# Edge key blocks in a hybrid attention trunk: products over 128 query columns instead of 256 with zeros

## The chip, the cores and the metric

The kernel runs on one core of one Trainium2 chip, in one launch. The metric is the device time of that core in microseconds (us), from the first instruction of the program to the last; lower is better. Five engines and the DMA queues matter in the text: TensorE (PE in the profile, its weight loads listed apart as PEld), VectorE (DVE), ScalarE (ACT), GpSimd (POOL), and SyncE (SP, which issues nearly all DMAs).

## What is computed

The reference is a trunk of two layers over 1024 tokens of width 1024, in float32. Each layer projects the normalised input to three groups of attention heads that run beside each other, normalises each group's output, multiplies by one output matrix and adds the result to the stream; a SwiGLU feed-forward part follows.

```
def reference(...):
    for l in range(2):
        h = rms_norm(x, g_attn[l]) * (1 + sc_a) + sh_a
        qa, ka, va, qb, kb, vb, qc, kc, vc = split_cols(h @ w_in[l], IN_SPLITS)
        ya = neighborhood_attention(qa, ka, va, rpb_na[l])         # 4 heads, 8 x 16 window on a 16 x 64 grid
        yb = sliding_window_attention(qb, kb, vb, sink_sw[l], t5)  # 6 heads, |i - j| <= 128
        yc = axial_attention(qc, kc, vc, gq_ax[l], gk_ax[l])       # 6 heads, dense
        y = concat([rms_norm(ya), rms_norm(yb), rms_norm(yc)])
        x = x + gt_a * (y @ w_o[l])
        h = rms_norm(x, g_ffn[l]) * (1 + sc_f) + sh_f
        gate, up = split_cols(h @ w_gu[l])
        x = x + gt_f * ((silu(gate) * up) @ w_down[l])
    return rms_norm(x, g_final)
```

In the neighbourhood group a query sees 8 grid rows of 64 tokens around its own, so a block of 128 queries (two grid rows) sees up to 9 rows, 576 keys. In the sliding group a block of 128 queries sees its own block of 128 keys and one block on either side, as far as there is one.

## The kernel before, in words

Products of float32 numbers are made from parts of type F32R: a number is rounded to a high part on ScalarE (`act.copy` into an F32R tile), and VectorE or GpSimd subtracts it from the original to get the low part. Such a pair is multiplied in two or three matmuls. Every matmul in the trace comes with a weight load of its own.

In a layer's attention part the work goes in pairs of query blocks: 24 pairs of the dense group C (6 heads by 4 pairs), 16 of the neighbourhood group A (4 heads by 4 pairs) and 24 of the sliding group B (6 heads by 4 pairs), in that order, in the list `stream`. Each pair, of 256 queries, goes through three steps:

- `qk`: the scores in PSUM (tiles `sC`, `sA`, `sB`), on VectorE the bias and the row's extreme (tile `rs`), on ScalarE the exponential with its sum (tile `pr`), then a reciprocal on VectorE and a scaling of the row on GpSimd;
- `turn`: blocks of 128 keys by 128 queries are transposed on TensorE into a PSUM tile `T`, from which `split_pt` makes the high and the low part (ScalarE, then VectorE) in the tiles `pt`;
- `pv`: for each key block `kc`, `products` multiplies the values `vs[:, kc]` as weights with the transposed rows as moving columns, the high and the low part one after the other, and adds up in a PSUM tile `pv` (two pairs share its 512 columns).

Most key blocks are seen by both query blocks of a pair, and their tiles hold 256 columns. An edge key block is seen by one of the two only: the key block before the pair by its left query block, the one behind by its right. In the neighbourhood group the two inner pairs of each head have two edge blocks (`PairA`, `self.inner`); in the sliding group pairs 1 and 2 of each head have two, pairs 0 and 3 one (`PairB`, `self.left`, `self.right`). These parts lie in tiles called `edge`. Before the change there are two `edge` tiles for the whole part, made once by `edges_make` with 256 columns for each side: the columns of the query block that does not see the key block are set to zero by GpSimd and stay so, and `next_edge` hands out the two tiles in turn. So every matmul of an edge block has 256 moving columns, as the others have.

With 2 matmuls (high and low) for each edge block there are 16 edge blocks in the neighbourhood group (32 matmuls) and 36 in the sliding group (72 matmuls) of a layer: 104, and 208 in the kernel.

In the attention part only GpSimd's instructions stand in the order of the source (`pin((pool,), True)`). For TensorE, VectorE, ScalarE and SP the order is laid down by the scheduler of the framework when the kernel is built, from its own picture of when each instruction is ready. Another shape of a few matmuls can therefore move other instructions too. All operations are issued through one helper, so that the profile gives line 49 for nearly all of them; the tiles' names tell them apart.

Of the kernel before, what the change touches and what calls it, by code (L numbers as in the profile page):

```python
# [76 lines left out]
def f32(ap):  # L77
    return ap.bitcast(F32)
# [7 lines left out]
def trunk(ctx: ExitStack, tc, A, C, out):  # L86
# [723 lines left out]
    for l in range(2):  # L810
# [379 lines left out]
        zA = [zA_tile() for _ in range(2)]  # L1190
        zB = [bz_tile() for _ in range(2)]
        gss = {23: gss_tile()}
        edge = []

        def edges_make():
            for _ in range(2):
                e = atp.tile([P, 2, 2, 256], F32R, name="edge", tag="edge", bufs=2)
                for z in range(2):
                    pool.memset(f32(e[:, z, 0, 128:256]), 0.0)
                    pool.memset(f32(e[:, z, 1, 0:128]), 0.0)  # L1200
                edge.append(e)

        edges_used = [0]

        def next_edge():
            edges_used[0] += 1
            return edge[edges_used[0] % 2]

        def edge_ap(e, z, left, right):
            flat = e[:, z, :, :].rearrange("p e q -> p (e q)")  # L1210
            if left and right:
                return flat.rearrange("p (a q) -> p a q", a=4)[:, 0:4:3, :]
            return flat[:, None, 0:128] if left else flat[:, None, 384:512]

        def pt_tile():
            return wp.tile([P, 4, 256], F32R, name="pt", tag="whl", bufs=8)
# [14 lines left out]
        class Pair:  # L1231
# [11 lines left out]
            def products(self, movs, part):  # L1243
                if part == 0:
                    if self.p % 2 == 0:
                        open_pv[0] = psV.tile([P, H], F32, name="pv", tag="V")
                    self.pvt = open_pv[0]
                cols = slice((self.p % 2) * 256, (self.p % 2) * 256 + 256)
                half = (len(movs) + 1) // 2
                for n, (kc, a, b) in enumerate(movs):  # L1250
                    if (n < half) != (part == 0):
                        continue
                    for i, mv in enumerate((a, b)):
                        pe.matmul(
                            self.pvt[:, cols], vs[:, kc, self.vh, :], mv,
                            start=(n == 0 and i == 0), stop=(n == len(movs) - 1 and i == 1),
                        )
                if part and self.p % 2:
                    self.combine()
# [68 lines left out]
        class PairA(Pair):  # L1328
# [64 lines left out]
            def pv(self, part):  # L1393
                k0 = {0: 0, 1: 1, 2: 3, 3: 4}[self.p]
                movs = [(k0 + i, self.pt[0][:, i, :], self.pt[1][:, i, :]) for i in range(4)]
                if self.inner:
                    e = self.e
                    movs.append((k0 - 1, e[:, 0, 0, :], e[:, 1, 0, :]))
                    movs.append((k0 + 4, e[:, 0, 1, :], e[:, 1, 1, :]))
                self.products(movs, part)  # L1400

        class GroupB:
# [18 lines left out]
        class PairB(Pair):  # L1421
# [64 lines left out]
            def pv(self, part):  # L1486
                k0, e = 2 * self.p, self.e
                movs = [(k0 + i, self.pt[0][:, i, :], self.pt[1][:, i, :]) for i in range(2)]
                if self.left:
                    movs.append((k0 - 1, e[:, 0, 0, :], e[:, 1, 0, :]))  # L1490
                if self.right:
                    movs.append((k0 + 2, e[:, 0, 1, :], e[:, 1, 1, :]))
                self.products(movs, part)


# [93 lines left out]
        for n in range(-AHEAD - 1, N + 1):  # L1589
            ahead = AHEAD if n + AHEAD < 40 else AHEAD_B  # L1590
            begin = range(done, min(n + ahead + 1, N))
            for i in range(2):
                if 0 <= n < N:
                    pairs[n].turn(i)
                while unfinished:
                    unfinished.pop(0)()
                if 0 <= n - 1 < N:
                    pairs[n - 1].pv(i)
                for m in begin:
                    if m < made:  # L1600
                        pairs[m].qk(i)
            done = max(done, min(begin.stop, made))
            while made < min(N, n + ahead + 2):
                for key, make in preload.get(made, []):
                    heads[key] = make()
                pairs[made] = stream[made][0]()
                made += 1
            for what in later.pop(n, []):
                what()
            if n == 50:  # L1610
                yq = qk_tile()
            if n == 8:
                edges_make()
            if n == 54:
                wst = [w_o_stage(k) for k in korder[:2]]
            if n in (55, 59):
                ki = (n - 55) // 4
                y_split(korder[ki], 0, yq[:, ki, 0:H], yq[:, ki, H:S])
            if n in (59, 61):
                w01.append(split_tile(wst.pop(0), 1, (atp, "pr", 6), dve))  # L1620
            if n == 60:
                t2 = [psS.tile([P, 2, H], F32, name="ps_o", tag="S") for _ in range(2)]
                pss = [t2[i // 2][:, i % 2, :] for i in range(NS)]
            if n in (61, 62):
                o_rows(0, w01[0], range(NS)[2 * (n - 61) : 2 * (n - 60)])
            if n in (63, 64):
                o_rows(1, w01[1], range(NS)[2 * (n - 63) : 2 * (n - 62)])
            if n == 62:
                wq = [w_rows(w_o, k * P, eng=dve) for k in korder[2:4]]
            m = n - 1  # L1630
            for end, (chunks, width) in norms.items():
                if begins[end] <= m <= end and (m - begins[end]) % 8 == 7:
                    i = (m - begins[end]) // 8
                    if end not in gss:
                        gss[end] = gss_tile()
                    for half in range(2):
                        what = lambda a=(chunks, gss[end], i, half): norm_sum(*a)
                        if m == N - 1:
                            what()
                        else:  # L1640
                            later.setdefault(n + 1 + half, []).append(what)
                    if m == end and end < N - 1:

                        def stats(end=end, width=width, n=n, chunks=chunks):
                            r = rstd_cols([gss[end]], width, 8, atp, psT, tag="T", newton=True)

                            def scale():
                                todo = norm_scale(chunks, r, psT, "T", (pool, pool))
                                for i, what in enumerate(todo):
                                    later.setdefault(n + 9 + i, []).append(what)  # L1650

                            later.setdefault(n + 8, []).append(scale)

                        later.setdefault(n + 5, []).append(stats)
# [693 lines left out]
```

## Time and profile before

| | |
|---|---|
| median of 3 runs | 2460.08 us (2459.95 to 2464.16) |
| profiled execution, its own time | 2460.14 us |
| its span, first to last instruction | 2458.4 us |
| TensorE busy | 2387.5 us, 97% |
| VectorE busy | 1819.2 us, 74% |
| ScalarE busy | 1227.1 us, 50% |
| GpSimd busy | 764.6 us, 31% |

A TensorE record covers a matmul's way through the array, so that records of neighbouring matmuls overlap. How fast matmuls follow each other is read from the distance of their starts (or of their ends, where the first of a group waited), not from the length of one record. Busy TensorE is therefore not TensorE at its limit.

In both layers the attention part runs at the same places of the program. By the first and the last record of the score tiles, the neighbourhood group's scores lie at 368 to 429 us of the span in the first layer and 1573 to 1633 us in the second, the sliding group's at 429 to 495 us and 1634 to 1699.5 us; products of both groups run on a little behind the scores, the last until 513 and 1717 us.

### The profile page before, as it was taken

The page shows a single profiled execution, that of the slowest core. Times are in us where ns is not written, and L with a number is a line of the kernel's source. Part 1 is how long each engine was busy: PE and PEld are TensorE (multiplying, and loading weights), DVE is VectorE, ACT ScalarE, POOL GpSimd, SP SyncE. Part 2 cuts the span into 40 slices and gives each one's busy share as a digit, 9 for nine tenths or more (in the row PEclk, how much of TensorE's full clock was granted, in tenths as well). Part 3 has the DMA queues.
Part 4 walks back from the last instruction along what each step waited for, and adds up shares of the span by engine and source line. Part 5 has one row for each costly group of instructions (what it writes and reads, how often), then busy time and mean ns, then how long its engine had stood idle before and what let it go on. Part 6 is the DMA issues. An engine that isn't in the chain of part 4 may idle for free.

```text
span 2458.4 us, 34300 instructions
## 1 busy us (share of the span) xinstructions
PE 2387.5 (97%) x12005; PEld 1991.2 (81%) x12005; DVE 1819.2 (74%) x2966; ACT 1227.1 (50%) x2306; POOL 764.6 (31%) x769
## 2 busy tenths in 40 slices
PE   8999999999999999999999999999999999999998
PEld 4787899878788787788787789987887888888886
DVE  5757999986967888586677679998688545446865
ACT  3422888954543333344543148888444343334443
POOL 1520445620244444300036124465004434430001
PEclk9999999999999999999999999999999999999999
DMA  8468205255245454596424851141624332229743
GB/s 285 149 188 282 56 6 145 57 165 160 86 142 173 158 178 152 163 274 193 152 85 116 279 165 27 48 148 50 206 86 141 119 121 95 99 96 296 209 134 110
DMA packets 285205, 356.04 MB, mean 145 GB/s; under 512 B 32996, under 2 KB 201532, under 8 KB 285032
## 3 DMA queue, kind: packets, MB, share of 16 engines
q1 hardware_dynamic: 277816, 341.12, 44.4%
q10 hardware_dynamic: 6912, 12.59, 1.6%
q8 instruction: 95, 1.56, 0.3%
q14 instruction: 78, 0.64, 0.1%
q0 software_dynamic: 304, 0.14, 0.0%
HBM read 269.62 MB, written 86.69 MB: 145 GB/s over the span
## 4 chain that ended last, share of the span: by engine, by line
PE 73%; DVE 9%; DMA 6%; issue 4%; ACT 4%; POOL 2%; SPq 1%; ACTq 0%; POOLq 0%; DVEq 0%
PE ps_w L49 28%; PE ps_d L49 14%; PE ps_o L49 7%; PE pv L49 6%; PE ps_ab L49 6%; PE T L49 4%; PE sC L49 3%; DMA wmt<-in_w_mod_dram 1%; SPq L49 1%; ACT pr L49 1%; DMA zAd<-zt 1%; PE sA L49 1%; DMA zt<-skA 1%; PE ps_v L49 1%; PE ps_c L49 1%
## 5 line engine op out<-in xcount | busy, mean ns | idle before, releaser
L49 PE MATMUL ps_d<-wpt 128*128 128x512 f32 x1848 | 424.3, 390 | 2.4 <-ACT wpt L49 2.1
L49 PEld LDWEIGHTS ps_d<-wpt 128*128 128x128 f32 x1848 | 345.6, 188 | 76.4 <-issue 3.0
L49 POOL TENSOR_SCALAR pr<-pr,rs 128x1024 f32<-128x1024 f32 (+4 forms) x252 | 206.9, 823 | 309.8 <-DVE rs L49 293.2
L49 POOL TENSOR_TENSOR sg<-sg,u 128x512 f32<-128x512 f32 x86 | 124.6, 1451 | 356.3 <-ACT sg L49 117.9
L49 PE MATMUL pv<-pt,vs 128*128 128x256 f32 x1216 | 202.0, 296 | 7.8 <-DVE rs L49 2.3
L49 DVE TENSOR_TENSOR pt<-T,pt 128x512 fp32r<-128x512 f32 x304 | 199.5, 680 | 11.4 <-ACT pt L49 9.9
L49 ACT CAST wpt<-w 128x512 fp32r<-128x512 f32 x154 | 95.7, 621 | 196.4 <-PE ps_d L49 175.1
L49 ACT CAST pt<-T 128x512 fp32r<-128x512 f32 x304 | 170.1, 586 | 43.3 <-PE T L49 41.7
L49 PE MATMUL T<-identr,pr 128*128 128x128 f32 x1288 | 187.0, 273 | 2.2 <-ACT rb L49 1.0
L49 PEld LDWEIGHTS pv<-pt,vs 128*128 128x128 f32 x1216 | 161.2, 189 | 23.0 <-DVE y L49 7.6
L49 DVE SCALAR_TENSOR_TENSOR acc<-wmt,condT,acc 128x512 f32<-128x512 f32 (+1 forms) x98 | 118.4, 1218 | 81.6 <-DMA wmt<-in_w_mod_dram 81.3
L49 DVE TENSOR_TENSOR wpt<-w,wpt 128x512 fp32r<-128x512 f32 x154 | 108.9, 707 | 84.4 <-ACT wpt L49 84.4
L49 ACT COPY u<-ps_w 128x512 f32<-128x512 f32 x128 | 75.1, 587 | 192.5 <-PE ps_w L49 192.4
L49 PEld LDWEIGHTS T<-identr,pr 128*128 128x128 f32 x1288 | 152.6, 140 | 22.0 <-issue 3.2
L49 POOL TENSOR_TENSOR wpt<-ws,wpt 128x512 fp32r<-128x512 f32 x80 | 112.8, 1410 | 180.3 <-ACT wpt L49 140.0
L49 ACT CAST wpt<-ws 128x512 fp32r<-128x512 f32 x176 | 107.8, 622 | 62.6 <-issue 28.4
L49 DVE TENSOR_TENSOR wpt<-ws,wpt 128x512 fp32r<-128x512 f32 x96 | 83.9, 885 | 59.0 <-ACT wpt L49 58.9
L49 DVE TENSOR_TENSOR wpt<-graw,wpt 128x512 fp32r<-128x512 f32 x154 | 110.0, 714 | 18.6 <-ACT wpt L49 18.5
L49 DVE TENSOR_REDUCE rs<-sC 128x1 f32<-128x1024 f32 x96 | 116.4, 1218 | 6.1 <-PE sC L49 5.7
L49 PE MATMUL ps_w<-h22h,wpt 128*128 128x512 f32 x352 | 111.7, 399 | 5.4 <-ACT sg L49 3.5
L49 DVE TENSOR_TENSOR ws<-wr 128x512 f32<-128x512 f32 x88 | 79.9, 910 | 48.6 <-POOL wpt L49 45.4
L49 ACT CAST whi<-wst 128x1024 fp32r<-128x1024 f32 x74 | 77.3, 1048 | 73.4 <-PE ps_o L49 47.9
(287 smaller groups left out, 6040.5 us busy)
## 6 DMA issues: line engine op xcount, KB each, us to landing
wr<-in_w_gu_dram SPq DMA_DIRECT2D x92, 512.0 KB, 4.2
gpd<-sg SPq DMA_DIRECT2D x154, 256.0 KB, 4.5
graw<-gpd SPq DMA_DIRECT2D x76, 512.0 KB, 3.7
w<-in_w_down_dram SPq DMA_DIRECT2D x110, 256.0 KB, 5.3
wmt<-in_w_mod_dram SPq DMA_DIRECT2D x48, 512.0 KB, 5.7
qk<-qkd SPq DMA_DIRECT2D x44, 512.0 KB, 7.2
wst<-in_w_o_dram SPq DMA_DIRECT2D x32, 512.0 KB, 3.5
wmt<-in_w_mod_dram SPq DMA_DIRECT2D x64, 256.0 KB, 3.6
```

The source lines that it names most:

```text
L49: ins = op(*args, **kwargs)
```

## The change

The `edge` tile holds 128 columns for each side instead of 256, it is taken anew for each pair from a ring of three, and the zeros with their GpSimd instructions are gone. In `products` an edge block comes with a column offset (0 for the left query block, 128 for the right), and its matmuls take 128 moving columns and write the 128 columns of `pv` that belong to this query block. Since the matmuls of one sum no longer cover the same columns, the build's check of groups is switched off for them. The order of the key blocks in a sum stays: those with 256 columns first, the first of which starts the sum over all 256 columns.

```
-        edge = []
-
-        def edges_make():
-            for _ in range(2):
-                e = atp.tile([P, 2, 2, 256], F32R, name="edge", tag="edge", bufs=2)
-                for z in range(2):
-                    pool.memset(f32(e[:, z, 0, 128:256]), 0.0)
-                    pool.memset(f32(e[:, z, 1, 0:128]), 0.0)
-                edge.append(e)
-
-        edges_used = [0]
-
         def next_edge():
-            edges_used[0] += 1
-            return edge[edges_used[0] % 2]
+            return atp.tile([P, 2, 2, P], F32R, name="edge", tag="edge", bufs=3)
 
         def edge_ap(e, z, left, right):
-            flat = e[:, z, :, :].rearrange("p e q -> p (e q)")
-            if left and right:
-                return flat.rearrange("p (a q) -> p a q", a=4)[:, 0:4:3, :]
-            return flat[:, None, 0:128] if left else flat[:, None, 384:512]
+            return e[:, z, 0 if left else 1 : 2 if right else 1, :]
...
-                cols = slice((self.p % 2) * 256, (self.p % 2) * 256 + 256)
                 half = (len(movs) + 1) // 2
-                for n, (kc, a, b) in enumerate(movs):
+                for n, (kc, a, b, *at) in enumerate(movs):
                     if (n < half) != (part == 0):
                         continue
+                    c0 = (self.p % 2) * 256 + sum(at)
+                    cols = slice(c0, c0 + (P if at else 256))
                     for i, mv in enumerate((a, b)):
                         pe.matmul(
                             self.pvt[:, cols], vs[:, kc, self.vh, :], mv,
                             start=(n == 0 and i == 0), stop=(n == len(movs) - 1 and i == 1),
+                            skip_group_check=True,
                         )
...
-                    movs.append((k0 - 1, e[:, 0, 0, :], e[:, 1, 0, :]))
-                    movs.append((k0 + 4, e[:, 0, 1, :], e[:, 1, 1, :]))
+                    movs.append((k0 - 1, e[:, 0, 0, :], e[:, 1, 0, :], 0))
+                    movs.append((k0 + 4, e[:, 0, 1, :], e[:, 1, 1, :], P))
...
                 if self.left:
-                    movs.append((k0 - 1, e[:, 0, 0, :], e[:, 1, 0, :]))
+                    movs.append((k0 - 1, e[:, 0, 0, :], e[:, 1, 0, :], 0))
                 if self.right:
-                    movs.append((k0 + 2, e[:, 0, 1, :], e[:, 1, 1, :]))
+                    movs.append((k0 + 2, e[:, 0, 1, :], e[:, 1, 1, :], P))
...
-            if n == 8:
-                edges_make()
```

TensorE, VectorE, ScalarE and SP run as many instructions as before; GpSimd runs 16 fewer (8 in each layer), the zeros. On TensorE the scheduler lays the two groups' instructions down in another order from the middle of the neighbourhood group on. The first place is there, in the first layer: products of an inner pair (`pv<-pt` with 8 matmuls and `pv<-edge` with 4), scores of later pairs (`sA`) and transposes (`T`). Before:

```order
L49 MATMUL pv<-edge,vs 128x256 x4
L49 MATMUL sA<-qk 128x288 x4
L49 MATMUL T<-identr,pr 128x128 x4
L49 MATMUL sA<-qk 128x288 x4
L49 MATMUL T<-identr,pr 128x128 x4
L49 MATMUL sA<-qk 128x288 x4
L49 MATMUL T<-identr,pr 128x128 x2
L49 MATMUL pv<-pt,vs 128x256 x8
L49 MATMUL pv<-edge,vs 128x256 x4
```

The same place on TensorE in the changed kernel:

```order
L49 MATMUL pv<-edge,vs 128x128 x4
L49 MATMUL sA<-qk 128x288 x4
L49 MATMUL T<-identr,pr 128x128 x4
L49 MATMUL sA<-qk 128x288 x4
L49 MATMUL T<-identr,pr 128x128 x4
L49 MATMUL sA<-qk 128x288 x2
L49 MATMUL pv<-pt,vs 128x256 x8
L49 MATMUL pv<-edge,vs 128x128 x4
L49 MATMUL sA<-qk 128x288 x2
```

The products have moved ahead of half of the last scores and of two transposes; no product or score is gone.

The second place is in the sliding group of the first layer, on TensorE, where pairs with one and with two edge blocks follow each other. `sB` are the scores. Before:

```order
L49 MATMUL pv<-pt,vs 128x256 x4
L49 MATMUL pv<-edge,vs 128x256 x2
L49 MATMUL pv<-pt,vs 128x256
L49 MATMUL sB<-qk 128x384 x2
L49 MATMUL T<-identr,pr 128x128 x4
L49 MATMUL pv<-pt,vs 128x256
L49 MATMUL sB<-qk 128x384 x2
L49 MATMUL pv<-pt,vs 128x256 x2
L49 MATMUL T<-identr,pr 128x128 x2
L49 MATMUL pv<-edge,vs 128x256 x4
```

The same place on TensorE in the changed kernel:

```order
L49 MATMUL pv<-pt,vs 128x256 x4
L49 MATMUL pv<-edge,vs 128x128 x2
L49 MATMUL pv<-pt,vs 128x256
L49 MATMUL sB<-qk 128x384 x4
L49 MATMUL T<-identr,pr 128x128 x4
L49 MATMUL pv<-pt,vs 128x256 x3
L49 MATMUL T<-identr,pr 128x128 x2
L49 MATMUL pv<-edge,vs 128x128 x4
L49 MATMUL sB<-qk 128x256 x2
```

Here the second couple of score matmuls has moved ahead of the four transposes, which now stand behind four score matmuls instead of two.

On GpSimd, in the dense group of the first layer, stood the zeros between the scalings of the rows:

```order
L49 TENSOR_SCALAR pr<-pr,rs 128x1024 x19
L49 MEMSET edge 128x128 x8
L49 TENSOR_SCALAR pr<-pr,rs 128x1024 x18
L49 TENSOR_TENSOR gss<-gss,gsq 128x512
L49 TENSOR_SCALAR pr<-pr,rs 128x1024 x2
```

In the changed kernel the scalings stand there without a break:

```order
L49 TENSOR_SCALAR pr<-pr,rs_1945 128x1024 x2
L49 TENSOR_SCALAR wst<-wst,rs_2010 128x1024 x2
L49 TENSOR_SCALAR pr<-pr,rs 128x1024 x37
L49 TENSOR_TENSOR gss<-gss,gsq 128x512
L49 TENSOR_SCALAR pr<-pr,rs 128x1024 x2
```

## Rows read from the trace of the kernel before

**Rows 1.** The page: busy time of engines; shares of the chain that ended last.

```profile
PE 2387.5 (97%) x12005; PEld 1991.2 (81%) x12005; DVE 1819.2 (74%) x2966; ACT 1227.1 (50%) x2306; POOL 764.6 (31%) x769
...
PE 73%; DVE 9%; DMA 6%; issue 4%; ACT 4%; POOL 2%; SPq 1%; ACTq 0%; POOLq 0%; DVEq 0%
```

**Rows 2.** Stretches: length, busy time of each engine, granted clock, DMA share, GB/s.

```profile
368.30:429.20 60.90, 59.89 (x467) 56.08 (x466) 56.37 (x157) 53.45 (x120) 30.45 (x52) 1.00 0.54 147
429.20:497.00 67.80, 62.98 (x432) 53.65 (x431) 62.08 (x219) 62.55 (x172) 44.56 (x85) 1.00 0.18 52
497.00:512.80 15.80, 14.52 (x90) 12.10 (x89) 15.08 (x22) 9.87 (x18) 4.64 (x4) 1.00 0.31 102
...
1634.00:1702.00 68.00, 63.26 (x435) 54.16 (x434) 62.55 (x220) 63.02 (x174) 45.05 (x86) 1.00 0.18 52
```

**Rows 3.** The tile edge: count, shortest/median/longest ns, first and last start.

```profile
L49 PEld LDWEIGHTS pv<-edge,vs x208: 186/189/193, 391.9 to 1716.9; 128*128 128x128 f32 x104
L49 PE MATMUL pv<-edge,vs x208: 278/283/388, 392.0 to 1717.0; 128*128 128x256 f32 x104
```

**Rows 4.** TensorE groups, 429.2:497 (first five), then edge groups of 368.3:429.2 and 497:512.8.

```profile
L49 PE MATMUL T<-identr,pr 128*128 128x128 f32 x142 | 22.6, 274 | 0.6 <-DVE pt L49 0.2
L49 PE MATMUL pv<-pt,vs 128*128 128x256 f32 x108 | 20.9, 302 | 2.1 <-DVE rs L49 1.2 <-ACT pt L49 0.4 <-DVE pt L49 0.2
L49 PE MATMUL sB<-qk 128*128 128x384 f32 x72 | 20.2, 365 | 0.3
L49 PE MATMUL pv<-edge,vs 128*128 128x256 f32 x62 | 11.6, 293 | 0.4 <-DVE edge L49 0.4
L49 PE MATMUL sB<-qk 128*128 128x256 f32 x24 | 5.7, 321 | 1.1 <-DVE rs L49 1.1
...
L49 PE MATMUL pv<-edge,vs 128*128 128x256 f32 x24 | 3.9, 283 | 0.0
...
L49 PE MATMUL pv<-edge,vs 128*128 128x256 f32 x18 | 3.3, 291 | 0.0
```

**Rows 5.** TensorE in order of time (start us, length us), 905 and 1600 us.

```profile
905.10 0.39 PE L49 MATMUL ps_w<-ht2l,wpt 128*128 128x512 f32 x1
905.32 0.61 PE L49 MATMUL ps_w<-ht2h,wpt 128*128 128x512 f32 x2
905.78 0.39 PE L49 MATMUL ps_w<-ht2l,wpt 128*128 128x512 f32 x1
...
1601.12 0.64 PE L49 MATMUL pv<-edge,vs 128*128 128x256 f32 x4
1601.60 0.38 PE L49 MATMUL T<-identr,pr 128*128 128x128 f32 x2
```

**Rows 6.** TensorE at 1607 us, in order of time; weight loads of two groups.

```profile
1607.25 1.70 PE L49 MATMUL ps_st<-onesr,gss 128*128 128x1 f32 x14
1608.82 0.37 PE L49 MATMUL pv<-pt,vs 128*128 128x256 f32 x1
...
L49 PEld LDWEIGHTS pq<-identr,qn 128*128 128x128 f32 x128 | 12.6, 140 | 2.1 <-issue 0.2
L49 PEld LDWEIGHTS ps_st<-onesr,gss 128*128 128x128 f32 x96 | 11.6, 192 | 0.3
```

**Rows 7.** TensorE at 93 us, in order of time: transposes of an F32R tile.

```profile
93.38 0.67 PE L49 MATMUL pq<-identr,qn 128*128 128x128 f32 x6
93.89 0.34 PE L49 MATMUL pk<-identr,qn 128*128 128x128 f32 x2
```

**Rows 8.** Waits at 429 to 513 us: total us, times, longest.

```profile
DVE rs L49 <- ACT pr L49: 2.8, 9, 0.5
...
ACT edge L49 <- PE pv L49: 0.6, 1, 0.6
```

**Rows 9.** GpSimd in order of time at 301 us, with the idle time before.

```profile
301.75 1.23 POOL L49 MEMSET edge<- 128x128 f32 x8
303.37 1.13 POOL L49 TENSOR_SCALAR pr<-pr,rs 128x1024 f32<-128x1024 f32 x1 [0.39 <-DVE rs L49]
```

## The prediction

> **What bounds the kernel now.** I read four views, from the whole down to single matmuls. The page first: TensorE is busy for 97% of the span and holds 73% of the chain that ended last [rows 1]. So a change that takes columns off TensorE can reach the end, but how much is to be read from the stretches in which the 208 edge matmuls lie. The view of stretches is the second. It separates two kinds. In the neighbourhood stretch of the first layer (60.90 us) TensorE is busy for 59.89 and no other engine for more than 56.37: TensorE sets the time. In the sliding stretch (67.80 us) ScalarE is busy for 62.55 and VectorE for 62.08, TensorE's records for 62.98: three engines at the same height. A third stretch, 497 to 512.8 us, holds the last products among the output matmuls. The granted clock is 1.00 of 2.4 GHz in all of them, and the second layer reads alike (68.00 us, 63.02 for ScalarE) [rows 2].
>
> The third view is the distance of starts, because the records overlap. Three matmuls of 512 columns take 905.78 - 905.10 = 0.68 us, 227 ns each. Four edge matmuls of 256 columns take 1601.60 - 1601.12 = 0.48 us, 120 ns each. Two transposes into T take 0.38 us, one record of which is 0.27, so 110 ns apart [rows 4, 5]. With these I work out what TensorE needs in the sliding stretch of the first layer, the 384 columns of sB at the middle between 120 and 227, 173: 142 x 110 + 108 x 120 + 72 x 173 + 62 x 120 + 24 x 120 = 51.4 us [rows 4]. That is well under 67.8, though the records look like 62.98: there TensorE waits within its chain, and ScalarE and VectorE are the fuller ones.
>
> The fourth view is what else can set the distance of two matmuls: the weight load. Each edge matmul has one, 208 loads for 208 matmuls, of 189 ns in the median [rows 3]. The sums for the norms (ps_st) show what remains if there is next to nothing to stream: one moving column, a new weight block each, and 14 of them take 1608.82 - 1607.25 = 1.57 us, 112 ns each, with loads of 192 ns [rows 6].
>
> **The change part by part.** *Half the columns of 208 matmuls.* A matmul of 512 columns takes 227 ns and one of 256 takes 120, so by columns alone one of 128 would take 120 - 107/2 = 66 ns. I don't take that. The loads stay, of the same length as those of ps_st, and these hold a matmul to 112 ns. So I take 120 - 112 = 8 ns for each. Bounds: at best 66 ns (54 less), at worst 227, which is what four times 128 columns would take (107 more); the trace has no product of F32R tiles narrower than 256 columns, so neither is excluded by a row of its own kind.
>
> Where the 8 ns lie, for one layer: 24 edge matmuls start in the neighbourhood stretch, 62 in the sliding and 18 in the last one, 104 together [rows 4]. In the first and the last TensorE is the fullest or among output matmuls that queue for it: 42 x 8 ns = 0.34 us on the path. In the sliding stretch 62 x 8 ns = 0.50 us, of which I count half, 0.25, because ScalarE and VectorE set much of the time there (none at the least, all at the most). Two layers: 2 x (0.34 + 0.25) = 1.2 us.
>
> Here a rule of the Trainium skill can be weighed. The page "TensorE: Matmul & The Clock Gate", section "LDWEIGHTS (loading the stationary operand)", says that a load takes its number of columns over 1.2 in ns, so 107 for 128 columns; the 112 ns of ps_st agree within 5%. By the page the gain would be 13 ns a matmul, 1.9 us in the same sum.
>
> *No zeros.* GpSimd's 8 memsets take 1.23 us at 301.75 us, in the dense group. The scaling behind them still waits 0.39 us for VectorE's reciprocal [rows 9]. So VectorE hides them, and I cost their absence at nothing; with that cover gone it would be 1.2 us a layer.
>
> *Three edge tiles in a ring instead of two.* Before, ScalarE's write into an edge tile waited once for the products of an earlier pair, 0.6 us in the sliding group [rows 8]. With three it should not. What is late next on ScalarE and VectorE is their exchange over the rows (2.8 us of VectorE waiting for ScalarE's pr [rows 8]). Nothing at the least, 0.6 a layer at the most; I take nothing. The split writes as many elements to the contiguous target as it did to the strided one: I count no difference.
>
> *Another order.* TensorE's order differs from the middle of the neighbourhood group on, and with it those of ScalarE and VectorE. The change section shows that products and scores exchange places by a few matmuls; nothing is added. Its cost can't be read from the trace before. Bounds: the fullest of the other engines has 67.80 - 62.55 = 5.25 us free in the sliding stretch, TensorE 1.0 in the neighbourhood one [rows 2]. A perfect order could win 6.3 us a layer, 12.5 in all, and I take the same for the other side. The value that I take is nothing: both orders have the same steps ahead and keep the pairs in the same sequence.
>
> The sum: -1.2 us against the profiled execution's own 2460.14 us, which is 2458.9. The median of the three runs, 2460.08, is 0.06 lower and changes nothing.
>
> **The rivals.** *The order makes it slower.* The place is the sliding group, where in the new order four score matmuls stand ahead of four transposes that had two ahead of them before. The transposes then come 2 x 173 = 0.35 us later, and ScalarE's split and VectorE's behind it start later. It decides as soon as ScalarE has nothing else ready, and ScalarE has only 5.25 us of free time in the stretch. If half of the 48 pairs of the two layers lose 0.35 us, that is 8.4 us: 2467.3. For it: three engines equally full, each wait is passed on. Against: groups of four score matmuls of 384 columns occur 8 times in each order, in the new one always with transposes behind, before 6 times of 8; the places differ more than their number. The opposite, an order that wins as much as half of the bound, 6.3 us, gives 2452.6; nothing in the rows favours it.
>
> *Narrow F32R products run in several passes.* The price is 107 ns for each: 2 x 42 x 0.107 = 9.0 us on the path, and in the sliding stretch 2 x 62 x 0.107 = 13.3, half of it 6.6: 2475.7; between 2469 and 2482 as the sliding stretch hides all or nothing (its need on TensorE would be 51.4 + 6.6 = 58.0, still under ScalarE's 62.55). For it: nothing narrower has run there as a product. Against: transposes of an F32R tile, 128 columns with a load each, follow each other at (93.89 - 93.38)/6 = 85 ns [rows 7], which leaves no room for four passes.
>
> *The load is faster than 112 ns.* The same row carries it: 85 ns at 128 columns with 128 weight columns. Then each edge matmul gains 35 ns, 2 x (42 x 0.035 + half of 62 x 0.035) = 5.1 us: 2455.0. Against: the loads of those transposes last 140 ns, those of the edge matmuls 189 like the 192 of ps_st [rows 3, 6], so they are of the slow kind. The same page of the Trainium skill has a rule for this, in "Back-to-back issue gap": a stream of loads and matmuls at 128 columns runs at some 81 ns a matmul. The 85 ns agree with it, the 112 do not; by 81 ns the time would be 2454.4.
>
> **How the numbers follow.** A measurement of this kernel tells a difference of about 0.2%, 4.9 us, from none: faster is below 2455.2, slower above 2465.0. My forecast, the floor of the loads with an order that is worth little either way, has 0.66; its own range is 2456 to 2463. The order costs more than that: 0.11, of which two thirds lie above 2465.0. The order wins more: 0.07, mostly below 2455.2. Several passes: 0.10, all slower. Faster loads: 0.06, half of it below. So slower is 0.10 + 0.07 = 0.17; faster 0.05 + 0.03 and 0.02 from the forecast's own edge, 0.10; the rest, 0.73, is within. The range 2454 to 2467 leaves out the several passes, the upper end of the worse order and the lower end of the better one, some 0.17. The predicted time is that of the likeliest case, 2458.9.
>
> **What would show it right or wrong.** In the changed profile four edge matmuls in a row should start 112 ns apart, with loads of 189 ns; 66 to 85 ns would show faster loads, about 227 several passes. The neighbourhood stretch should be shorter by 0.2 to 0.3 us, the sliding one by less than 1 us or changed either way by the order, which would show as more or less idle time of ScalarE and VectorE at the same busy time. The stretches without attention should be alike within their noise. The prediction is wrong if the sliding stretch changes by more than 2.5 us a layer, or if the distance of the edge matmuls is not between 106 and 120 ns.

## The result and the profile after

The changed kernel takes 2474.53 us in the median of 5 runs (2472.01 to 2477.47), the kernel before beside it 2460.08 us (2455.93 to 2466.20). The ratio is 1.0049 [1.0037, 1.0061]: slower, by some 12 us. The forecast was 2458.9 us.

The page of the changed kernel has TensorE busy for 11 us more than before, in as many matmuls, though 208 of them have half their columns; the other engines differ by 6 us or less [rows 1]:

```profile
PE 2398.9 (97%) x12005; PEld 1995.9 (81%) x12005; DVE 1825.1 (74%) x2966; ACT 1228.7 (50%) x2306; POOL 760.1 (31%) x753
```

The edge products themselves do what was forecast. By tile (ns: least, median, most) their loads are as long as those with 256 columns, 192 against 189 ns in the median, and their records a little shorter, 274 against 283 [rows 3]. The starts inside such groups are 110 ns apart in the median, where the loads alone take 112 [rows 6]. There is one exception: behind another product or a score the second of a group starts some 60 ns after the first (47 of 50 such groups), and only from there on are they 109 to 115 ns apart. The loads of four start in steps of 110 to 118 ns all the same:

```profile
L49 PEld LDWEIGHTS pv<-edge,vs x208: 186/192/333, 397.8 to 1731.6; 128*128 128x128 f32 x104
L49 PE MATMUL pv<-edge,vs x208: 220/274/415, 397.9 to 1731.7; 128*128 128x128 f32 x104
...
402.20 0.56 PE L49 MATMUL pv<-edge,vs 128*128 128x128 f32 x4
...
402.08 0.54 PEld L49 LDWEIGHTS pv<-edge,vs 128*128 128x128 f32 x4
```

The time is lost between the matmuls, in three stages of each layer. The table gives the lengths of a layer's stages from the first score or product matmul of a stage to that of the next, in us of the profiled execution, for layer 1 and layer 2. C is the dense group, A the neighbourhood group, B the sliding group, o the output projection with the last products.

| kernel | C | A | B | o | span |
|---|---|---|---|---|---|
| before | 136.0 / 136.0 | 60.9 / 60.9 | 68.3 / 68.0 | 99.3 / 99.3 | 2458.4 |
| after | 138.9 / 139.2 | 62.0 / 62.3 | 70.1 / 71.3 | 98.8 / 98.8 | 2475.7 |

C, A and B are longer, o a little shorter. That is +5.3 us in the first layer and +7.4 in the second, 12.7 together. The other 4.6 us between these two executions lie in stretches without attention, whose length also changes from run to run with the number of short falls of the clock; I don't ascribe them to the change.

The view of stretches shows A and B of the first layer and B of the second, which answer to [rows 2] (start and end, length; busy time and count of TensorE, its loads, VectorE, ScalarE and GpSimd; granted clock; DMA share and GB/s):

```profile
374.20:436.20 62.00, 61.12 (x467) 56.11 (x465) 57.54 (x157) 53.91 (x120) 30.65 (x52) 1.00 0.53 144
436.20:506.30 70.10, 64.09 (x445) 54.75 (x443) 67.21 (x224) 64.06 (x175) 45.98 (x86) 1.00 0.18 50
...
1647.70:1719.00 71.30, 65.45 (x446) 56.23 (x444) 67.32 (x224) 64.23 (x175) 46.05 (x86) 0.98 0.18 49
```

The clock is full in both stretches of the first layer, so their loss is one of order and waits. In the second layer's B it is 0.98: 3.4 us of it ran at 1.2 GHz. In B VectorE is now busy for 67.21 of 70.10 us; before it was 62.08 of 67.80 [rows 2].

The dense group, of whose instructions the change touches none but GpSimd's zeros, has lost 2.9 and 3.2 us. All of it goes within some 8 us, 21 us behind its first score. The chain of waits there (start, length, what) in the changed kernel:

```profile
252.38 0.58 ACTq L49
...
253.00 3.67 DMA qkd<-qko
...
256.80 1.23 DVE rs L49
...
258.10 1.21 ACT pr L49 x2
...
259.36 1.99 PE sC L49 x4
```

A store of the projections (qko to DRAM) is in the chain: VectorE writes a small tile `rs` only when this DMA has landed. The timeline shows the price, in brackets what an engine waited and for whom; first VectorE and TensorE after, then the same two places before:

```profile
256.80 2.36 DVE L49 TENSOR_REDUCE rs<-sC 128x1 f32<-128x1024 f32 x2 [1.22 <-DMA qkd<-qko]
...
259.36 1.99 PE L49 MATMUL sC<-qk 128*128 128x512 f32 x4 [2.06 <-ACT pr L49]
```

```profile
252.51 2.35 DVE L49 TENSOR_REDUCE rs<-sC 128x1 f32<-128x1024 f32 x2
...
255.01 1.19 PE L49 MATMUL sC<-qk 128*128 128x512 f32 x4 [0.70 <-ACT pr L49]
```

TensorE waits 2.06 us where it waited 0.70. Behind the wait its clock falls, as the view of stretches shows for layer 1 and layer 2 after; in the same place before it was 1.00:

```profile
256.40:263.00 6.60, 4.54 (x20) 3.76 (x19) 5.22 (x8) 3.55 (x7) 1.27 (x2) 0.74 0.01 5
1467.60:1475.00 7.40, 4.99 (x22) 4.03 (x21) 5.50 (x9) 4.48 (x8) 2.24 (x2) 0.77 0.13 34
```

```profile
253.00:259.60 6.60, 5.90 (x41) 5.16 (x40) 6.46 (x11) 5.69 (x11) 2.44 (x3) 1.00 0.23 81
```

0.74 over 6.6 us is 3.4 us at the lower level, 1.2 GHz, and the rest at 2.4.

Why does `rs` wait for a store? The tiles of the attention part lie in one pool that ends at a fixed address and grows downwards, so a tile's place is that end less everything taken behind it. A ring of two `edge` tiles took 8192 bytes of each partition; one of three half as wide takes 6144. Every tile taken earlier lies 2048 bytes higher: the `rs` ring moves from 156544 to 157056, just below the second qko buffer (157824 to 161920), to 158592 to 159104, inside of it. That buffer is still being read by the last two stores of the projections when the first scores are done. (At its old place the ring lies in the first qko buffer, and no wait shows for the stores from there.) So two things came with the change beside the narrower products: another order and another place. The experiments take them apart.

### The profile page after: what moved, and what is told of

Its sections match the earlier page's. It is cut to its first block, busy times and chain, and to the rows that moved or that the text cites. A ratio compares the mean times of both kernels' runs of the same rounds, so it can differ in the third digit from the quotient of the medians.

```text
span 2475.7 us, 34264 instructions
## 1 busy us (share of the span) xinstructions
PE 2398.9 (97%) x12005; PEld 1995.9 (81%) x12005; DVE 1825.1 (74%) x2966; ACT 1228.7 (50%) x2306; POOL 760.1 (31%) x753
## 4 chain that ended last, share of the span: by engine, by line
PE 73%; DVE 10%; DMA 6%; issue 5%; ACT 3%; POOL 2%; SPq 1%; POOLq 0%; ACTq 0%; DVEq 0%
PE ps_w L49 27%; PE ps_d L49 14%; PE ps_o L49 7%; PE ps_ab L49 6%; PE pv L49 6%; PE T L49 4%; PE sC L49 3%; DMA wmt<-in_w_mod_dram 2%; PE ps_c L49 1%; DMA zAd<-zt 1%; DVE acc L49 1%; DMA zt<-skA 1%; PE ps_v L49 1%; PE sA L49 1%; ACT pr L49 1%
## 5 line engine op out<-in xcount | busy, mean ns | idle before, releaser
L49 PEld LDWEIGHTS ps_d<-wpt 128*128 128x128 f32 x1848 | 345.5, 188 | 76.5 <-issue 3.0
L49 DVE TENSOR_TENSOR pt<-T,pt 128x512 fp32r<-128x512 f32 x304 | 199.5, 680 | 10.3 <-ACT pt L49 8.8
L49 ACT CAST wpt<-graw 128x512 fp32r<-128x512 f32 x154 | 95.0, 617 | 48.1 <-DMA graw<-gpd 43.0
```

The lines of the kernel that those rows point to most:

```text
L49: ins = op(*args, **kwargs)
```

## The experiments

All kernels but e1 hold the order of the attention part by a table: for TensorE, ScalarE, VectorE and SP the sequence of the instructions (1980, 391, 537 and 53 of a layer, the same in both), each tied to the one before it. 381 places on TensorE, 142 on VectorE and 69 on ScalarE differ between the two orders, none on SP. In short:

```
-            ins = op(*args, **kwargs)
+            ins = note(self, op(*args, **kwargs))
...
+            row = [made[id(eng)][n + int(k)] for n, k in enumerate(steps_)]
+            for first, then in zip(row, row[1:]):
+                tc.add_manual_dep(then, first.name, ...)
```

The place is set by the size of a filler at the pool's end. e1 to e8 were timed against the kernel before (11 or 12 runs each), e9 to e12 ran once. Narrow stands for edge products over 128 columns, wide for 256. Their stages, as above, are those of one profiled execution each, whose time can lie some us off the median (e1's: 2463.05 against 2470.07). So the table tells where time went, and the ratios tell how much:

| kernel | C | A | B | o | span |
|---|---|---|---|---|---|
| e1 narrow, new order, old place | 136.0 / 136.0 | 62.0 / 62.0 | 70.1 / 71.7 | 98.9 / 98.9 | 2461.3 |
| e2 narrow, old order, new place | 137.4 / 140.8 | 60.8 / 60.8 | 68.0 / 68.0 | 99.3 / 99.3 | 2461.3 |
| e3 narrow, old order, old place | 136.0 / 136.0 | 60.8 / 60.8 | 68.0 / 68.0 | 99.3 / 99.3 | 2459.4 |
| e4 wide, old order, new place | 137.4 / 137.8 | 60.9 / 60.9 | 68.3 / 68.0 | 99.3 / 99.3 | 2459.1 |
| e5 wide, new order, old place | 136.0 / 136.1 | 62.1 / 62.1 | 70.6 / 70.4 | 98.8 / 98.8 | 2461.2 |
| e6 narrow, new order in A only | 136.1 / 136.0 | 62.0 / 62.0 | 69.2 / 69.1 | 99.8 / 99.3 | 2463.5 |
| e7 narrow, new order, four steps late | 136.1 / 136.1 | 62.0 / 62.0 | 69.9 / 69.2 | 100.8 / 100.8 | 2462.1 |
| e8 narrow, old order, these steps early | 136.0 / 136.0 | 60.8 / 60.8 | 71.0 / 71.2 | 98.3 / 98.3 | 2463.0 |
| e9 as e3, 32 columns | 136.0 / 136.0 | 60.8 / 60.8 | 68.0 / 68.0 | 99.3 / 99.3 | 2457.5 |
| e10 TensorE's order new | 136.1 / 136.1 | 63.3 / 63.3 | 73.8 / 76.8 | 100.4 / 99.5 | 2477.5 |
| e11 TensorE's and VectorE's new | 136.1 / 136.0 | 65.7 / 65.7 | 76.5 / 77.4 | 98.6 / 98.6 | 2486.7 |
| e12 ScalarE's new | 136.1 / 136.1 | 61.8 / 61.8 | 75.0 / 75.0 | 99.3 / 99.3 | 2479.7 |

**e1: the change with the tiles at their old place.**

```
-        pad(atp, 384)
+        pad(atp, 384 + 2048)
```

> The changed kernel with 2048 bytes of padding at the end of the attention part's tile pool, so that its tiles rs, pr, zA and so on lie at the addresses that they had in the kernel before; the order of all instructions is the changed kernel's. Placement theory: in the changed kernel the first tile rs of the dense group lies on the buffer that the last store of the projections is still read from, VectorE waits 1.2 us for that store, TensorE 1.6 us behind it, and TensorE then runs 3.4 us at half clock; 3.0 us per layer. With the padding 2474.5 - 6.0 = 2468.5 (2467 to 2471), and no wait for that store. Theory of several passes for narrow products: nothing changes, 2474.5. Theory that narrow products lower the clock: nothing changes, 2474.

Measured: 2470.07 against 2462.45 us, ratio 1.0026 [1.0016, 1.0036], within the range expected. C is back at 136.0, A and B stay long. The timeline of VectorE at C's start has no wait any more:

```profile
252.86 2.35 DVE L49 TENSOR_REDUCE rs<-sC 128x1 f32<-128x1024 f32 x2
```

**e2: the change with the order of before.** After with the table of the old order.

> The changed kernel (narrow products, ring of three edge tiles, its own addresses), with the instructions of TensorE, VectorE, ScalarE and SyncE from the dense group to the output projection held in the order of the kernel before. Order theory: the new order costs some 2.4 us per layer between the start of the neighbourhood group and the feed-forward part; 2474.5 - 4.8 = 2469.7 (2468 to 2472), with the wait for the store still there. Several passes: TensorE pays 107 ns for each narrow product whatever the order, 2474 or more. Clock theory: 2474.

Measured: 2466.53 us, 1.0016 [1.0006, 1.0025]. That is less than the range expected: the order's share was put too low. A and B are back, C stays long.

**e3: both back.** e1's filler and e2's table; what is left of the change is the narrower products, the ring of three and the missing zeros.

> The changed kernel with the padding and with the order of the kernel before: what is left of the change is the narrow products, the ring of three and the missing zeros. Placement and order theory: 2460.1 - 1.2 = 2458.9 (2456 to 2462). Several passes: 2475. Narrow products lower the clock: 2465 to 2470, with more stretches at half clock than before.

Measured: 2463.11 us, beside 2462.45 for the kernel before; 0.9999 [0.9990, 1.0008]: no difference from before. (The time is above the range expected, 2456 to 2462, but so is that of the kernel before beside it.) A and B are 0.1 and at most 0.3 us shorter. That is all that the narrower products give.

**e4: products of 256 columns at the new place.** The kernel before with its order held and its two edge tiles cut to 6144 bytes, the zeros of both sides being shared:

```
-                e = atp.tile([P, 2, 2, 256], F32R, name="edge", tag="edge", bufs=2)
+                e = atp.tile([P, 2, 3, P], F32R, name="edge", tag="edge", bufs=2)
...
+        def edge_mv(e, z, side):
+            return e[:, z, side : side + 2, :].rearrange("p a q -> p (a q)")
...
+                    movs.append((k0 - 1, edge_mv(e, 0, 0), edge_mv(e, 1, 0)))
+                    movs.append((k0 + 4, edge_mv(e, 0, 1), edge_mv(e, 1, 1)))
```

> The kernel before with wide products (256 columns, half of them zeros) and its own order, but the two edge tiles hold the zeros once between the left and the right side, 6144 bytes in all as in the changed kernel, so that the tiles rs, pr, zA lie at the changed kernel's addresses. Placement theory: the wait for the store appears, 2460.1 + 6.0 = 2466 (2464 to 2468). The other theories: 2460.

Measured: 2467.05 us, 1.0014 [1.0004, 1.0024]. The wait is there without any narrow product:

```profile
252.50 2.35 DVE L49 TENSOR_REDUCE rs<-sC 128x1 f32<-128x1024 f32 x2 [1.24 <-DMA qkd<-qko]
...
255.06 1.19 PE L49 MATMUL sC<-qk 128*128 128x512 f32 x4 [2.08 <-ACT pr L49]
```

Here the clock stayed at 1.00 behind it in both layers, and C is 137.4 and 137.8: the wait alone costs 1.4 and 1.8 us, in the first layer just what TensorE waits more (2.08 - 0.70). Where the clock falls as well, C becomes 2.9 to 4.8 us longer (after, and e2's second layer). The falls go with the wait: in the profiled executions of all kernels here the clock falls within C in three of the six places with the wait (after, e2, e4) and in none of the 22 without it. A fall adds 1.4 us or more to what the wait costs.

**e5: products of 256 columns in the new order.** The kernel before with the table of the new order.

> The kernel before with its wide products, zeros and addresses, but the instructions of TensorE, VectorE, ScalarE and SyncE from the dense group to the output projection held in the changed kernel's order. Order theory: slower than before by what the first experiment still showed, a ratio of 1.0026 (1.0015 to 1.0035), with the neighbourhood stretch some 1.2 us and the sliding stretch some 2 us longer in each layer. Theory that only narrow products make that order slow (they fit it badly): 1.000.

Measured: 2465.52 against 2461.16 us, 1.0016 [1.0006, 1.0026]. A, B and o are those of e1 within 0.5 us, but for e1's second B, in which the clock fell. So the order costs without narrow products too.

**e6: the new order up to the first score of the sliding group, then the old.**

> Narrow products at the old addresses; the new order up to the first score matmul of the sliding group, the old order from there. Theory that the order costs where it stands: 1.2 us per layer in the neighbourhood stretch (62.0 instead of 60.8), none behind it, 2.4 us in all, ratio 1.001. Theory that the sliding stretch is late because the neighbourhood group handed on its lateness: the sliding stretch is longer too, 1.002 or more.

Measured: 2462.99 us, 1.0004 [0.9994, 1.0014], which alone decides nothing. By the stretch A has its 62.0, so the loss there comes from A's own rows. B was longer than e3's by 1.2 and 1.1, with a fall of the clock in both layers; the lines are the first layer's:

```profile
368.50:430.50 62.00, 61.14 (x465) 56.10 (x464) 57.49 (x156) 53.97 (x120) 30.45 (x52) 1.00 0.52 144
430.50:499.70 69.20, 64.85 (x439) 55.42 (x437) 62.71 (x219) 63.13 (x172) 45.10 (x85) 0.98 0.19 51
```

So that part can't be put down to the order. No B in the old order (before, e2, e3, e4, e9: ten stretches) has a fall; of the twelve in after, e1 and e5 to e8, seven have one. Stages are therefore to be compared at full clock.

**e7 and e8: four steps of VectorE.** The view by tile shows a difference of B between e1 and e3 on VectorE: the steps that make the low parts of the output projection's operand (qk from y) run four times inside B in the new order, once in the old.

```profile
L49 DVE SCALAR_TENSOR_TENSOR qk<-y,vecs,qk x4: 737/1254/1782, 467.6 to 489.6; 128x512 fp32r<-128x512 f32 x4
```

```profile
L49 DVE SCALAR_TENSOR_TENSOR qk<-y,vecs,qk x1: 732/732/732, 470.4 to 470.4; 128x512 fp32r<-128x512 f32 x1
```

e7 keeps the new order, but with the second to fifth of these steps at their places of the old; e8 keeps the old order, with them at the places of the new.

> Narrow products at the old addresses in the new order, except that four of the five low parts of the output projection's input (VectorE, tile qk from y) stand as late as in the old order, behind the sliding group's work instead of within it. Theory that these low parts (0.74 to 1.78 us each on the fullest engine) make the sliding stretch longer: it falls from 70.1 and 71.7 to 68.5 or less, the stretch behind it grows by some 0.4, ratio 1.0015 to 1.002 instead of 1.0026. Theory that TensorE's order does it: the sliding stretch stays at 70 or more.

> Narrow products at the old addresses in the old order, except that the five low parts stand on VectorE where the new order has them, within the sliding group's work. Theory of the low parts: the sliding stretch grows from 68.0 to 69.5 or more, the one behind shrinks by some 0.4, ratio 1.001 to 1.0015. Theory of TensorE's order: both stay as they are in the old order, 1.000.

Measured: e7 2466.63 us, 1.0024 [1.0015, 1.0033]; e8 2462.83 us, 1.0005 [0.9993, 1.0016]. In e7 VectorE is relieved in B. Its first B (69.90) holds a fall of the clock; the second, at full clock, is 69.2, that is 0.9 less than e1's first at full clock (70.1). But o grows by 1.9 us. In e8 VectorE is fuller in B than in e3 by 2.8 us and the stretch longer by 3, with a fall of the clock in both layers. The lines are B in e7 (layer 1, then 2), e8 and e3 (layer 1):

```profile
430.90:500.80 69.90, 65.58 (x447) 56.26 (x444) 64.18 (x221) 63.82 (x175) 45.67 (x86) 0.98 0.17 50
1635.04:1704.22 69.18, 64.73 (x446) 54.70 (x445) 63.95 (x221) 63.90 (x175) 45.65 (x86) 1.00 0.18 50
```

```profile
429.50:500.50 71.00, 64.15 (x437) 54.97 (x435) 65.42 (x223) 63.81 (x174) 45.30 (x86) 0.98 0.18 50
```

```profile
428.70:496.70 68.00, 62.81 (x437) 53.53 (x435) 62.66 (x220) 63.07 (x174) 45.10 (x86) 1.00 0.19 52
```

In e8, B + o is 169.3 against 167.3 in e3, but with the falls in it, and the ratio can't be told from none: that the early steps cost something in the old order is not shown. Taking them out of the new order shortens B and lengthens o by more (B + o of 170.0 in e7's second layer against 169.0 in e1's first). My theory expected the time to fall with them, to 1.0015 to 1.002; it did not. Where they stand in B in the new order they do hold up TensorE, as the next section shows.

**e9: 32 columns.** e3 with 32 moving columns in each edge matmul; 96 of the 128 queries get nothing from their edge blocks, so part of the computation is left out.

```
-                    cols = slice(c0, c0 + (P if at else 256))
+                    cols = slice(c0, c0 + (32 if at else 256))
                     for i, mv in enumerate((a, b)):
+                        mv = mv[:, 0:32] if at else mv
```

> Old order and old addresses, and each edge product takes only the first 32 of its 128 query columns (the other 96 columns get nothing from the edge key blocks). Floor theory (the weight load holds a product to about 112 ns): edge products in a row still start 110 to 112 ns apart and the neighbourhood stretch stays at 60.8. Streaming theory (columns set the distance): some 26 to 40 ns apart, 24 x 75 ns = 1.8 us less in the neighbourhood stretch, 59.0. Several passes: as floor at 32 columns.

Measured: 2459.3 us in one run, the kernel before beside it 2460.31, and A and B to a tenth those of e3. Four edge matmuls and their loads in the timeline, and by tile the loads:

```profile
396.25 0.52 PE L49 MATMUL pv<-edge,vs 128*128 128x32 f32 x4
...
396.13 0.54 PEld L49 LDWEIGHTS pv<-edge,vs 128*128 128x128 f32 x4
...
L49 PEld LDWEIGHTS pv<-edge,vs x208: 186/192/193, 391.7 to 1716.0; 128*128 128x128 f32 x104
```

Four loads take 0.54 us at 32 columns, 0.54 at 128 and, in the kernel before, 0.55 at 256:

```profile
1601.00 0.55 PEld L49 LDWEIGHTS pv<-edge,vs 128*128 128x128 f32 x4
```

Behind another product or a score the second matmul of a group starts 28 ns after the first at 32 columns, 60 ns at 128 and 119 at 256: this distance goes with the columns. The later ones are 112, 112 and 120 ns apart: they do not, at 32 and 128 columns, and neither do the loads. Fewer columns have nothing to give here.

**e10, e11, e12: one engine's order at a time.** e3 with the table of the new order for TensorE alone, for TensorE and VectorE, and for ScalarE alone.

> Narrow products at the old addresses; TensorE alone in the new order, ScalarE and VectorE in the old one. Theory that TensorE's own order costs (products moved right behind scores wait for the PSUM bank that VectorE's add to y frees): the neighbourhood stretch is 61.5 to 62.5 instead of 60.8, the sliding stretch 69.5 or more. Theory that the orders of ScalarE and VectorE do it: 60.8 and 68.

> As the one before, with VectorE in the new order too and ScalarE in the old one. If TensorE's order is all, the stretches are as with TensorE alone; if VectorE's order adds to it, the sliding stretch goes to the 70.1 of the whole new order.

> As before, with ScalarE alone in the new order. TensorE's theory: 60.8 and 68 to 68.5. If ScalarE's order carries the loss: 62 and 70.

Measured, one run each: 2479.34, 2488.47 and 2481.56 us. All three are worse than e1 and e3, which have the same place and one whole order each, and B is longer than any theory had it (73.8 to 77.4 us). ScalarE in e12's B waits 8.0 us for VectorE's rs, in e3's 1.9. The orders of the engines fit each other, and the loss can't be put down to one engine's list.

## Why the prediction was wrong, and where it was right

**Half the columns of 208 matmuls: right.** The prediction put this at 8 ns each, by the floor of the weight loads, and 1.2 us in all. e3, in which nothing else is left but the ring of three and the missing zeros, is at 0.9999 [0.9990, 1.0008], which holds the 1.2 us and can't tell them from none; its A is 0.1 us shorter, its B by at most 0.3. e9 shows the floor itself. Faster loads would have shortened A by some 0.8 us, several passes would have made it longer by 2.6: neither is seen. The time that the rival of several passes gave, 2475.7 us, is near the measured one by accident; its mechanism is refuted, by e3 and by the second of a group, 60 ns behind the first. That distance is near the 66 ns that the prediction worked out by columns alone and below the 66 to 85 that it took as the sign of faster loads; but it is one of a group's distances alone, the loads keep theirs, and A does not become shorter by it.

**No zeros, a ring of three: right as costs of their own.** Both are in e3. But the ring's *size* was one of the two causes.

**Missing: where the tiles lie.** Here the prediction failed first: no step asked what addresses a smaller ring moves, and the sum has no term for it. The wait on the store costs 1.4 and 1.8 us in the two layers (e4), and with the clock's fall 2.9 and 3.2 in the profiled execution of the changed kernel. That the place is the cause is shown by taking the place alone (e4, 1.0014 [1.0004, 1.0024], 3.4 us; e2, 1.0016, 3.9 us) and by putting it back (after 1.0049, e1 1.0026, some 5.7 us). The views of before show no such wait in C, and could not: there the rs ring ended 768 bytes below the buffer that the store still reads. The prediction would have had to compare the tiles' addresses of both kernels, beside the order.

**"The value that I take is nothing" for another order: the other step that failed.** The order costs A 1.2 us, B about 2.1, and gives 0.4 back in o: 2.9 us a layer, 5.8 in all (e1: 1.0026, 6.4 us; e5, with wide products: 1.0016 [1.0006, 1.0026], some 4 us). It lies within the bounds of 6.3 us a layer, but for a loss these had no ground: the engines' free time bounds what an order can win, not what it can cost, and "I take the same for the other side" came without a reason. Nor is "the same steps ahead" evidence for nothing: what counts is which wait stands at the head of TensorE's queue. The first place of the change section shows how A loses. The timeline of TensorE in e1 and e3, same pairs:

```profile
394.35 0.60 PE L49 MATMUL T<-identr,pr 128*128 128x128 f32 x4
395.00 0.53 PE L49 MATMUL sA<-qk 128*128 128x288 f32 x2
395.60 1.21 PE L49 MATMUL pv<-pt,vs 128*128 128x256 f32 x8
396.65 0.56 PE L49 MATMUL pv<-edge,vs 128*128 128x128 f32 x4
397.04 0.49 PE L49 MATMUL sA<-qk 128*128 128x288 f32 x2
```

```profile
393.51 0.60 PE L49 MATMUL T<-identr,pr 128*128 128x128 f32 x4
394.17 0.80 PE L49 MATMUL sA<-qk 128*128 128x288 f32 x4
394.80 0.38 PE L49 MATMUL T<-identr,pr 128*128 128x128 f32 x2
394.94 1.20 PE L49 MATMUL pv<-pt,vs 128*128 128x256 f32 x8
395.97 0.56 PE L49 MATMUL pv<-edge,vs 128*128 128x128 f32 x4
```

In the old order two scores and two transposes stand between the scores and the products of a pair; in the new one the products come right behind two scores, and there their loads wait 0.30 us for VectorE's y, in e3 not at all. The waits of TensorE's loads in A, first in e1, then in e3 (us, times, longest):

```profile
PEld pv L49 <- DVE y L49: 1.9, 6, 0.4
PEld sA L49 <- DVE rs L49: 0.9, 3, 0.3
PEld pv L49 <- DVE pt L49: 0.7, 2, 0.4
PEld T L49 <- issue: 0.2, 1, 0.2
```

```profile
PEld pv L49 <- DVE y L49: 1.4, 4, 0.4
PEld T L49 <- issue: 1.1, 2, 0.7
PEld sA L49 <- DVE rs L49: 0.3, 1, 0.3
```

The products wait for VectorE to read the sums of the pairs before them out of `pv` (into y), the scores for VectorE to be done with the last ones; both more often in the new order. The waits for VectorE are 3.5 us against 1.7, the time without a named wait ("issue") 0.2 against 1.1: 0.9 us more in all, of the 1.2 that A is longer.

In B the waits of TensorE's loads differ little in sum (13.1 us in e1, 12.8 in e3), but those for VectorE rise from 7.8 to 10.3, and the two longest are new. Their lines in e1, with the steps of VectorE that stood before them, and what GpSimd did beside the second:

```profile
472.89 1.76 DVE L49 SCALAR_TENSOR_TENSOR qk<-y,vecs,qk 128x512 fp32r<-128x512 f32 x1
...
475.31 0.14 PEld L49 LDWEIGHTS T<-identr,pr 128*128 128x128 f32 x1 [1.34 <-DVE pt L49]
...
480.13 1.29 POOL L49 TENSOR_TENSOR y<-y,rb 128x512 f32<-128x512 f32 x1
...
480.19 1.78 DVE L49 SCALAR_TENSOR_TENSOR qk<-y,vecs,qk 128x512 fp32r<-128x512 f32 x1
...
482.62 0.53 PEld L49 LDWEIGHTS pv<-pt,vs 128*128 128x128 f32 x4 [1.36 <-DVE y L49]
```

Both steps are of the four that e7 and e8 move, and both last over 1.7 us instead of 0.74. Behind each, VectorE comes late to the instruction that TensorE waits for (pt, then y). All six stretches B in the whole new order (after, e1, e5) have these two waits, of 1.31 to 1.37 us; before and e3 have none above 0.95, and e7, without the steps, none above 0.81. At the same point of the work e1 is 0.6 us ahead of e3 before the first of them and 1.9 behind after the second. So this is where B falls behind in the new order. B also holds nine matmuls more (446 against 437), which is part of its length, and o becomes shorter by 0.4. That moving the steps wins the time back is refuted by e7: o pays for it.

**The rival of the order** named the sliding group, rightly, and missed A; its price, 8.4 us, is of the size of the 5.8 measured, but its account (the transposes come late for ScalarE) is not what the waits show: ScalarE waits for T as long in e1's B as in e3's (1.7 and 1.6 us), and it is VectorE that TensorE waits for. The nearness of its price is luck. The prediction's own bound for being wrong, 2.5 us in the sliding stretch, was passed in the second layer (71.3 against 68.0, with a fall of the clock in it) and not in the first (1.8 us); the distance of the edge matmuls held in the median, 110 ns.

**What stays open.** Which of the order's moves would have to be undone to win the 2.1 us of B back without losing them in o: the early steps alone are not it (e7), no engine's list alone carries the loss (e10 to e12), and e6 is too disturbed by the clock to say what the old rows of B give back. Why o becomes 1.9 us longer in e7 was not followed up. The two causes by their ratios make 6.4 + 3.9 = 10.3 of the 12.1 us that 1.0049 stands for; the rest is within the intervals. No version beat the kernel before: the best, e3, is the same.

## What to carry to other kernels

When a tile or a ring changes its size, list which other tiles move with it and what is still being read or written at their new addresses; the first uses of a stage show it as a wait for a DMA that has nothing to do with them. To judge a local edit in a kernel whose order a scheduler lays down, hold the order and the addresses fixed, and time order and place by themselves with the old instructions. Take columns off a matmul only down to the floor that its weight load sets, here 112 ns.

## What the hardware showed unexpectedly

The loads for products of F32R tiles with 32, 128 and 256 moving columns, each with a fresh weight block, are 111, 112 and 119 ns apart in the median. One wait of 2 us on TensorE can be followed by 3.4 us at the lower clock, but need not be: after 2.06 us it fell in the changed kernel, after 2.08 us in e4 it did not.

The same VectorE step, 128x512 from F32 to F32R, took 0.73 us in one place and 1.78 us in another of the same stage. The traces show what goes with it. In the profiles of before, after and e1 to e8 it runs 100 times. In 38 a GpSimd TENSOR_TENSOR of 1.3 us (y from y and rb, or gss from gss and gsq) was already running when it began: then it lasts 1.01 to 1.79 us and ends 0.55 us after that one. In the other 62, alone or beside a GpSimd TENSOR_SCALAR, it takes 0.73 to 0.75. So an order that puts the two beside each other costs VectorE up to 1.0 us each time.
